# Row sums of squared differences: the end of a row of x loaded last, and y's later loads in five even pieces

**The chip and the metric.** The kernel runs on one core of a Trainium2 chip. The metric is the time of one execution on the device in microseconds (us), from the chip's own clock. The profile comes from one execution each; its span runs from the first to the last instruction and is some 1.3 us shorter than the time. All runs told here are at a granted clock of 1.0.

## The reference

```python
def setup_inputs():
    batch, dim = 1024, 4096
    return {"x": np.random.randn(batch, dim).astype(np.float32),
            "y": np.random.randn(batch, dim).astype(np.float32), "axis": -1}

def reference(x, y, axis):
    return np.sum((x - y) ** 2, axis=axis).astype(np.float32)
```

Each of the 128 partitions holds 8 whole rows, that is 8 x 4096 = 32768 columns of x and as many of y. 33.55 MB must come in, and 4 KB go out.

## The kernel before

All loads are issued by SyncE on one queue, in the order in which they are needed. VectorE subtracts y from x in place as soon as a piece of both has landed, ScalarE squares the difference and sums it (an activation with an accumulator, which is read by a second small instruction), and a row that came in several pieces is completed on VectorE by a reduction over its partial sums. X and Y in SBUF hold six rows each; rows 6 and 7 take the place of rows 0 and 1, so their loads wait for the squares of those. The last 128 columns of row 3 (of y only, in this version) are kept back and loaded last of all; VectorE finishes them alone, with one subtraction and one fused square and sum, while ScalarE finishes row 7. Cuts are marked with dots; the comments are added here.

```python
    xw = [4096, 12288, 8192, 5472, 1280, 960, 320, 160]
    yw = [16256, 8192, 2624, 2784, 1344, 480, 480, 288]
    late, last = 128, 192
    LATE = 3
    halved = (1, 2, 3, 4)          # y loads whose columns are subtracted and squared in halves
    cut = (LATE + 1) * D - late
    ...
    ys += [(N - last, N), (cut, cut + late)]
    ...
    for j, (c0, c1) in enumerate(ys):
        final = j == len(ys) - 1
        wait_loaded(c1, landed_y[j][1])
        for piece in pieces_of(j, c0, c1):
            sub(*piece)                                   # VectorE, L175
            r = piece[0] // D
            if final:
                nc.vector.wait_ge(diffs, n["diffs"])
                nc.vector.tensor_tensor_reduce(...)       # VectorE, L204: the kept-back end of row 3
                continue
            square(*piece, where[piece])                  # ScalarE, L181
            ...
        if j == 4:
            for r in (4, 5, 6):
                complete(r)                               # VectorE, L188
    complete(7)
    nc.sync.wait_ge(sums, n["sums"])
    nc.sync.dma_start(out=ov, in_=results).then_inc(stored, 16)
```

Of the kernel before, what the change touches and what calls it, by code (L numbers as in the profile page):

```python
# [47 lines left out]
def kernel(tc, x, y, axis, out):  # L48
    nc = tc.nc
    P = nc.NUM_PARTITIONS  # L50
    F32 = mybir.dt.float32
    Square = mybir.ActivationFunctionType.Square
    mult, add = mybir.AluOpType.mult, mybir.AluOpType.add

    B, D = x.shape
    R = B // P
    N = R * D


    xv = x.rearrange("(p r) d -> p (r d)", p=P)  # L60
    yv = y.rearrange("(p r) d -> p (r d)", p=P)
    ov = out.rearrange("(p r) -> p r", p=P)


    H = 6 * D
    X = nc.alloc_sbuf_tensor("X", [P, H], F32).ap()
    Y = nc.alloc_sbuf_tensor("Y", [P, H], F32).ap()
    results = nc.alloc_sbuf_tensor("results", [P, R], F32).ap()



    xw = [4096, 12288, 8192, 5472, 1280, 960, 320, 160]
    yw = [16256, 8192, 2624, 2784, 1344, 480, 480, 288]
    late, last = 128, 192
    LATE = 3
    halved = (1, 2, 3, 4)
    cut = (LATE + 1) * D - late
    assert sum(xw) == N and sum(yw) == N - late - last
    xs, c = [], 0
    for w in xw:  # L80
        xs.append((c, c + w))
        c += w
    ys, c = [], 0
    for w in yw:
        ys.append((c, c + w))
        c += w
        if c == cut:
            c += late
    ys += [(N - last, N), (cut, cut + late)]

    prog = Program(nc, tc)
    stored = nc.alloc_semaphore("stored")
    diffs = prog.semaphore("diffs")
    acts = prog.semaphore("acts")
    sums = prog.semaphore("sums")
    n = dict(diffs=0, acts=0, sums=0)

    def home(c0, c1):
        h0 = c0 % H
        return slice(h0, h0 + c1 - c0)  # L100


    landed_x, landed_y = [], []
    freed = []

    def load(landed, src, dst, name, c0, c1):
        sem = prog.semaphore("%s%d" % (name, len(landed)))
        nc.sync.dma_start(out=dst[:, home(c0, c1)], in_=src[:, c0:c1]).then_inc(sem, 16)  # L108
        landed.append(((c0, c1), sem))

    order = []
    have = 0
    for c0, c1 in ys:
        while have < c1:
            order.append((landed_x, xv, X, "x") + xs[len([o for o in order if o[3] == "x"])])
            have = order[-1][5]
        order.append((landed_y, yv, Y, "y", c0, c1))

    todo = list(order)
    load(*todo.pop(0))  # L120
    prog.early(mybir.EngineType.SP)
    while todo and todo[0][5] <= H:
        load(*todo.pop(0))


    row_parts = [[] for _ in range(R)]
    def pieces_of(j, c0, c1):

        pieces = []
        while c0 < c1:  # L130
            e = min(c1, (c0 // D + 1) * D)
            if j in halved:
                h = (c0 + e) // 64 * 32
                pieces.append((c0, h))
                c0 = h
            pieces.append((c0, e))
            c0 = e
        return pieces

    for j, (c0, c1) in enumerate(ys):  # L140
        for piece in pieces_of(j, c0, c1):
            row_parts[piece[0] // D].append(piece)
    parts, where = None, {}
    total = sum(len(p) for p in row_parts if len(p) > 1)
    parts = nc.alloc_sbuf_tensor("parts", [P, total], F32).ap()
    k = 0
    for r, p in enumerate(row_parts):
        for piece in p:
            where[piece] = parts[:, k : k + 1] if len(p) > 1 else results[:, r : r + 1]
            k += len(p) > 1  # L150
    first = {}
    k = 0
    for r, p in enumerate(row_parts):
        if len(p) > 1:
            first[r] = k
            k += len(p)

    def parts_of(r, m):
        return parts[:, first[r] : first[r] + m]

    seen_x = [0]

    def wait_loaded(c1, ysem):

        waits = []
        while seen_x[0] < len(xs) and xs[seen_x[0]][0] < c1:
            waits.append(seen_x[0])
            seen_x[0] += 1
        nc.vector.wait_ge(ysem, 16)
        for k in waits:  # L170
            nc.vector.wait_ge(landed_x[k][1], 16)

    def sub(c0, c1):
        a = X[:, home(c0, c1)]
        nc.vector.tensor_sub(out=a, in0=a, in1=Y[:, home(c0, c1)]).then_inc(diffs, 1)  # L175
        n["diffs"] += 1

    def square(c0, c1, acc):
        a = X[:, home(c0, c1)]
        nc.scalar.wait_ge(diffs, n["diffs"])  # L180
        nc.scalar.activation(out=a, in_=a, func=Square, accum_out=acc).then_inc(acts, 1)  # L181
        n["acts"] += 1

    squared = {}

    def complete(r):
        nc.vector.wait_ge(acts, squared[row_parts[r][-1]])
        nc.vector.tensor_reduce(  # L188
            out=results[:, r : r + 1],
            in_=parts_of(r, len(row_parts[r])),  # L190
            axis=mybir.AxisListType.X,
            op=add,
        ).then_inc(sums, 1)
        n["sums"] += 1

    for j, (c0, c1) in enumerate(ys):
        final = j == len(ys) - 1
        wait_loaded(c1, landed_y[j][1])
        for piece in pieces_of(j, c0, c1):
            sub(*piece)  # L200
            r = piece[0] // D
            if final:
                nc.vector.wait_ge(diffs, n["diffs"])
                nc.vector.tensor_tensor_reduce(  # L204
                    out=Y[:, home(*piece)],
                    in0=X[:, home(*piece)],
                    in1=X[:, home(*piece)],
                    scale=1.0,
                    scalar=parts_of(r, 1),
                    op0=mult,  # L210
                    op1=add,
                    accum_out=results[:, r : r + 1],
                ).then_inc(sums, 1)
                n["sums"] += 1
                continue
            square(*piece, where[piece])
            squared[piece] = n["acts"]
            if r in (0, 1):

                nc.sync.wait_ge(acts, n["acts"])  # L220
                while todo and todo[0][5] <= H + (r + 1) * D:
                    load(*todo.pop(0))
                if r == 1:
                    while todo:
                        load(*todo.pop(0))
        if j == 4:
            for r in (4, 5, 6):
                complete(r)
    complete(7)

    nc.sync.wait_ge(sums, n["sums"])
    nc.sync.dma_start(out=ov, in_=results).then_inc(stored, 16)
    prog.close(nc.sync, stored, 16)
# [35 lines left out]
```

## Time and profile before

| | before |
|---|---|
| time, first three runs | 84.12 us (84.08 to 84.34) |
| the profiled run | 83.96 us, span 82.6 |
| bytes read | 33.55 MB, 406 GB/s over the span |
| loads | 8 of x, 10 of y |
| busy VectorE, ScalarE | 36.8 and 33.4 us |
| last load landed | 80.25 us |
| last reduction began | 80.99 us |

The table is to be read from the bottom up. What counts is when the last bytes arrive and how long the way from there to the last reduction is. The busy shares say nothing here, because both engines stand idle for the first 40 us, until the first long load of y has landed. The prediction below shows the lines. One line of the timeline that it only speaks of is this; its columns are start, length, engine, line, operation, operands, count, and the idle time before with what ended it:

```profile
73.28 4.80 DVE L175 TENSOR_TENSOR X<-X,Y 128x736 f32<-128x736 f32 x6 [0.37 <-DMA Y<-in_y_dram]
```

It shows VectorE working off a lump: the 2784 columns of y landed at 73.25, and six subtractions follow without a pause.

### The profile page before, as it was taken

What the parts mean: (1) busy time and instruction counts of PE and PEld (TensorE: products, weight loads), DVE (VectorE), ACT (ScalarE), POOL (GpSimd) and SP (SyncE); (2) the same over time, 40 slices, a digit from 0 to 9 for tenths busy, and PEclk for the clock granted to TensorE, in tenths of its full rate; (3) what the DMA queues carried; (4) which work ended last, traced back from release to release, by engine and by line L of the source; (5) the groups of instructions that cost most, each with busy time, mean ns of one, the idle gap of its engine ahead of it and who ended that gap; (6) DMA issues with size and microseconds to landing.
All of it is one profiled execution on the core that took longest, in us unless ns stands there. A gap on an engine that the chain in (4) does not pass through costs nothing.

```text
span 82.6 us, 136 instructions
## 1 busy us (share of the span) xinstructions
DVE 36.8 (45%) x27; ACT 33.4 (40%) x41; POOL 0.2 (0%) x4
## 2 busy tenths in 40 slices
DVE  0000000000000000000299999999189996989992
ACT  3300000000000000000000979889896999899991
POOL 0000000000000000000000000000000000000000
DMA  5998998888999991999599699969979799999960
GB/s 127 389 500 381 595 547 381 381 381 381 504 504 504 504 504 63 441 504 504 254 508 508 286 476 508 476 286 508 423 339 509 339 437 440 426 402 416 395 220 2
DMA packets 2736, 33.56 MB, mean 406 GB/s; under 512 B 432, under 2 KB 1328, under 8 KB 1712
## 3 DMA queue, kind: packets, MB, share of 16 engines
q1 hardware_dynamic: 2736, 33.56, 95.9%
HBM read 33.55 MB, written 0.00 MB: 406 GB/s over the span
## 4 chain that ended last, share of the span: by engine, by line
DMA 63%; SPq 16%; DVE 12%; ACT 4%; issue 1%
DMA Y<-in_y_dram 63%; SPq L108 16%; DVE X L175 11%; ACT X L181 4%; DVE Y L204 0%; DVE results L188 0%; SPq L220 0%; DVE results L204 0%
## 5 line engine op out<-in xcount | busy, mean ns | idle before, releaser
L175 DVE TENSOR_TENSOR X<-X,Y 128x2048 f32<-128x2048 f32 (+10 forms) x21 | 36.2, 1780 | 44.3 <-DMA Y<-in_y_dram 44.3
L181 ACT ACTIVATE X<-X 128x2048 f32<-128x2048 f32 (+9 forms) x20 | 31.2, 1559 | 46.1 <-DVE X L175 46.0
L181 ACT ACTIVATION_READ_ACCUMULATOR X<-X 128x1 f32 x20 | 3.7, 186 | 0.0
L181 ACT ACT_TABLE_LOAD x1 | 1.3, 1283 | 1.4 <-PEq L19 1.4
L188 DVE TENSOR_REDUCE results<-parts 128x1 f32<-128x2 f32 (+2 forms) x4 | 0.4, 152 | 0.0
L204 DVE CUSTOM_DVE_ANT_0 Y<-X,parts 128x128 f32<-128x128 f32 x1 | 0.4, 352 | 0.0
L250 POOL MEMSET const-bfloat16-1.0<- 128x1 bf16 x1 | 0.1, 101 | 0.0
L250 POOL MEMSET const-uint8-127<- 128x1 uint8 x1 | 0.1, 101 | 0.0
L250 POOL MEMSET const-float32-0.0<- 128x1 f32 x1 | 0.1, 98 | 0.2 <-issue 0.2
L250 POOL MEMSET const-float32-1.0<- 128x1 f32 x1 | 0.1, 98 | 0.0
L204 DVE DVE_READ_ACCUMULATOR2_ANT results<- 128x1 f32 x1 | 0.1, 83 | 0.0
## 6 DMA issues: line engine op xcount, KB each, us to landing
Y<-in_y_dram SPq DMA_DIRECT2D x1, 8128.0 KB, 39.0
X<-in_x_dram SPq DMA_DIRECT2D x1, 6144.0 KB, 20.2
X<-in_x_dram SPq DMA_DIRECT2D x1, 4096.0 KB, 48.3
Y<-in_y_dram SPq DMA_DIRECT2D x1, 4096.0 KB, 57.5
X<-in_x_dram SPq DMA_DIRECT2D x1, 2736.0 KB, 13.3
X<-in_x_dram SPq DMA_DIRECT2D x1, 2048.0 KB, 7.1
Y<-in_y_dram SPq DMA_DIRECT2D x1, 1392.0 KB, 19.0
Y<-in_y_dram SPq DMA_DIRECT2D x1, 1312.0 KB, 16.1
```

Of the source, the lines that this page charges most:

```text
L108: nc.sync.dma_start(out=dst[:, home(c0, c1)], in_=src[:, c0:c1]).then_inc(sem, 16)
L175: nc.vector.tensor_sub(out=a, in0=a, in1=Y[:, home(c0, c1)]).then_inc(diffs, 1)
L181: nc.scalar.activation(out=a, in_=a, func=Square, accum_out=acc).then_inc(acts, 1)
L188: nc.vector.tensor_reduce(out=results[:, r : r + 1], in_=parts_of(r, len(row_parts[r])), axis=mybir.AxisListType.X, op=add,).then_inc(sums, 1)
L204: nc.vector.tensor_tensor_reduce(out=Y[:, home(*piece)], in0=X[:, home(*piece)], in1=X[:, home(*piece)], scale=1.0, scalar=parts_of(r, 1), ...
L250: nc = _bacc.Bacc("TRN2", target_bir_lowering=False, num_devices=1)
```

## The change

Its intent is to smooth the last fifteen microseconds. The end of row 3 of x is kept back like that of y, so that the last pair of loads is small on both sides. One load of 6816 columns of x runs ahead, and y follows in five loads of about 1350 columns. Each of them, and the 768 columns after them, is subtracted and squared in halves. The number of loads stays at 18.

```diff
--- before.py
+++ after.py
@@ -69,24 +69,25 @@
 
 
 
-    xw = [4096, 12288, 8192, 5472, 1280, 960, 320, 160]
-    yw = [16256, 8192, 2624, 2784, 1344, 480, 480, 288]
-    late, last = 128, 192
+
+    xw = [4096, 12160, 8192, 6816, 768, 608]
+    yw = [16256, 8192, 1344, 1312, 1440, 1376, 1344, 768, 288, 320]
+    late = 128
     LATE = 3
-    halved = (1, 2, 3, 4)
+    halved = (1, 2, 3, 4, 5, 6, 7)
     cut = (LATE + 1) * D - late
-    assert sum(xw) == N and sum(yw) == N - late - last
-    xs, c = [], 0
-    for w in xw:
-        xs.append((c, c + w))
-        c += w
-    ys, c = [], 0
-    for w in yw:
-        ys.append((c, c + w))
-        c += w
-        if c == cut:
-            c += late
-    ys += [(N - last, N), (cut, cut + late)]
+
+    def pieces(widths):
+        spans, c = [], 0
+        for w in widths:
+            spans.append((c, c + w))
+            c += w
+            if c == cut:
+                c += late
+        assert c == N
+        return spans + [(cut, cut + late)]
+
+    xs, ys = pieces(xw), pieces(yw)
 
     prog = Program(nc, tc)
     stored = nc.alloc_semaphore("stored")
@@ -109,12 +110,12 @@
         landed.append(((c0, c1), sem))
 
     order = []
-    have = 0
-    for c0, c1 in ys:
-        while have < c1:
-            order.append((landed_x, xv, X, "x") + xs[len([o for o in order if o[3] == "x"])])
-            have = order[-1][5]
-        order.append((landed_y, yv, Y, "y", c0, c1))
+    xk = 0
+    for piece in ys:
+        while xk < len(xs) and (xs[xk][0] < piece[1] if xk < len(xs) - 1 else piece == ys[-1]):
+            order.append((landed_x, xv, X, "x") + xs[xk])
+            xk += 1
+        order.append((landed_y, yv, Y, "y") + piece)
 
     todo = list(order)
     load(*todo.pop(0))
@@ -160,12 +161,15 @@
 
     seen_x = [0]
 
-    def wait_loaded(c1, ysem):
+    def wait_loaded(c1, ysem, final):
 
         waits = []
-        while seen_x[0] < len(xs) and xs[seen_x[0]][0] < c1:
+        while seen_x[0] < len(xs) - 1 and xs[seen_x[0]][0] < c1:
             waits.append(seen_x[0])
             seen_x[0] += 1
+        if final:
+            assert seen_x[0] == len(xs) - 1
+            waits.append(seen_x[0])
         nc.vector.wait_ge(ysem, 16)
         for k in waits:
             nc.vector.wait_ge(landed_x[k][1], 16)
@@ -195,7 +199,7 @@
 
     for j, (c0, c1) in enumerate(ys):
         final = j == len(ys) - 1
-        wait_loaded(c1, landed_y[j][1])
+        wait_loaded(c1, landed_y[j][1], final)
         for piece in pieces_of(j, c0, c1):
             sub(*piece)
             r = piece[0] // D
@@ -223,7 +227,7 @@
                 if r == 1:
                     while todo:
                         load(*todo.pop(0))
-        if j == 4:
+        if j == 6:
             for r in (4, 5, 6):
                 complete(r)
     complete(7)
```

## The prediction

> **What bounds the kernel now.** I began with the page: its busy shares, the forty slices and the chain that ended last.
>
> ```profile
> DVE 36.8 (45%) x27; ACT 33.4 (40%) x41; POOL 0.2 (0%) x4
> DMA  5998998888999991999599699969979799999960
> GB/s 127 389 500 381 595 547 381 381 381 381 504 504 504 504 504 63 441 504 504 254 508 508 286 476 508 476 286 508 423 339 509 339 437 440 426 402 416 395 220 2
> DMA 63%; SPq 16%; DVE 12%; ACT 4%; issue 1%
> ```
>
> The two engines that compute work less than half of the span, the 16 DMA engines from the second slice to the last but one. Most of the chain is DMA. The 16% of SyncE's queue is issue time that lies beside transfers already queued: in the windows 40 to 50 us and 50 to 60 us, where it falls, the DMA moved 442 and 432 GB/s, no less than elsewhere. So the kernel is 33.55 MB at the rate of the DMA, and then a tail. The end of the chain shows the tail:
>
> ```profile
> 66.94 13.12 DMA Y<-in_y_dram
> 80.05 0.02 issue
> 80.08 0.57 DVE X L175 x2
> 80.65 0.03 issue
> 80.67 0.35 DVE Y L204
> 81.03 0.01 DVE results L204
> 81.03 0.12 DVE results L188
> ```
>
> The chain names 80.05 us. That is the last load but one, 192 columns of y. By the trace's landing records the last, 128 columns, lands at 80.25; VectorE had not come to it then. From the data at 80.05 follow two subtractions, the fused square and sum, and the reduction of row 7, which is through at 81.15; the store of the results takes the rest up to 82.6. Which engine is late just before? The timeline answers for both:
>
> ```profile
> 79.58 1.06 DVE L175 TENSOR_TENSOR X<-X,Y 128x288 f32<-128x288 f32 x3 [0.15 <-DMA Y<-in_y_dram]
> 79.97 0.19 ACT L181 ACTIVATION_READ_ACCUMULATOR X<-X 128x1 f32 x1
> 80.08 0.44 ACT L181 ACTIVATE X<-X 128x288 f32<-128x288 f32 x1
> 80.42 0.19 ACT L181 ACTIVATION_READ_ACCUMULATOR X<-X 128x1 f32 x1
> 80.52 0.35 ACT L181 ACTIVATE X<-X 128x192 f32<-128x192 f32 x1
> 80.77 0.19 ACT L181 ACTIVATION_READ_ACCUMULATOR X<-X 128x1 f32 x1
> 80.95 0.08 DVE L204 DVE_READ_ACCUMULATOR2_ANT results<- 128x1 f32 x1
> 80.99 0.16 DVE L188 TENSOR_REDUCE results<-parts 128x1 f32<-128x8 f32 x1
> ```
>
> VectorE still waits for data at 79.58, so it has caught up. ScalarE does not wait: its activations follow each other from about 72.9 us, with only their accumulator reads between. The 192 columns were subtracted at 80.08 + 0.36 = 80.44, and ScalarE takes them at 80.52, at most some 0.06 us late. It ends at 80.96, VectorE's fused operation and its accumulator read end at 81.03: the two branches into the last reduction are nearly even.
>
> **What the Trainium skill says.** "DMA: Bandwidth & Descriptors", section "Where 436 GB/s comes from", puts the ceiling at 435 GB/s. The trace agrees: the 8192 columns of y before 60.27 us took 9.72 us, that is 8192 x 128 x 4 B / 9.72 us = 431 GB/s. There is no rate left to win on large loads. Section "Why small descriptors are slow (HBM only)" speaks of a fixed overhead per packet; the gaps between landings below show a small one. "VectorE: DVE Perf Modes", section on the TRN2 errata, gives (N+151)/0.96 ns for an fp32 tensor_tensor: 2291 ns for 2048 columns, where the trace has 2287, and 291 for 128, where it has 285. "ScalarE: Activation LUTs", section "What ACT_TABLE_LOAD costs", gives 186 ns + 0.833 per column and an overlap of about 93 ns: 1892 for 2048, where the trace has 1910.
>
> **The change, part by part.**
>
> *Loads.* Before there are 8 of x and 10 of y, after 7 and 11: 18 both times, with the same bytes. I took the gaps between landings, in order of issue, as what each load costs: 8192 columns 9.72 us, 5472 6.49, 2624 3.17, 1344 1.61, 960 1.16, 480 0.60, 320 0.41, 288 0.40, 192 0.26, 160 0.23, 128 0.20. A line through the 13 gaps after y's 8192 columns is 0.038 us + 1.180 ns per column, with no point off by more than 0.03. In such a model the end of the stream depends on the number of loads and the sum of columns, and neither changes: the last landing stays at 80.25. If I take the measured gaps for each new size instead, interpolating where there is none, the 13 new ones add to 20.05 us against 19.99 for the old, but they begin 0.15 us sooner, since the 128 columns of x moved to the end come out of the second load: 80.16. So the transfers give 0 to 0.1 us.
>
> *When the loads are issued.* After the fifth load everything waits for the squares of row 1 (at 53.4 us) in both kernels: the new third load of x also reaches beyond row 0's room. Data runs until 60.27, and the last load was wholly issued at 72.98, 7 us before it landed. With 13 loads behind the wait again, I expect no starvation.
>
> *Rows 4 and 5*, four halves of 2048: unchanged, 8.90 us of VectorE from 60.15 instead of 60.29, free at 69.05.
>
> *The middle.* Five y loads of 1344, 1312, 1440, 1376, 1344 replace 2624, 2784, 1344. x's 6816 land first, at 60.12 + 0.04 + 8.04 = 68.2. Then y lands at 69.82, 71.41, 73.15, 74.81 and 76.43 by the line. VectorE needs for two halves about 2 x (0.07 us + 1.0417 ns x half), the 0.07 being what is left of the 8.90 us for four 2048s after their duration: 1.54, 1.51, 1.64, 1.57 and 1.54. Every piece is done before the next arrives. Before, the 2784 came in one lump at 73.25 and gave 4.80 us of subtraction in a row, and a backlog for ScalarE. Now VectorE is done at 78.0 with these and has paid its three reductions (some 0.2 us, from 77.99 to 78.18 before) by 78.2; the next data come at 78.3. ScalarE's pitch of about 0.75 us per 672 (76.61 to 77.35 to 78.11) keeps up with 1.6 us for two. This removes waiting that lay under the DMA; the part of it at the end was 0.06 us.
>
> *The end.* x 768, y 768, x 608, y 288, y 320, x 128, y 128 land at 77.38, 78.32, 79.08, 79.46, 79.87, 80.06 and 80.25. VectorE: 768 in halves 78.35 to 79.3; 288 from 79.49; 320 from 79.90, free for the next at 79.90 + 0.07 + 0.333 = 80.30; the last 128 from 80.30 instead of 80.36 (80.08 + 0.28). That is 0.06 us off the VectorE branch, with one subtraction of 128 after the last data where there were 192 and 128. But ScalarE now squares 320 columns last, not 192. Its data are ready at 79.90 + 0.49 = 80.39, it starts at 80.42, and at the old distance from start to end of accumulator read (80.96 - 80.52 = 0.44 for 192, plus 128 x 0.833 ns = 0.55) it ends at 80.97, where it was 80.96. So the reduction starts where it did, near 81.0. If the loads really end 0.1 us sooner, all of it moves by 0.1.
>
> Sum: transfers 0 to -0.1, tail 0 to -0.06, both branches considered. I take -0.08 of 84.12, that is 84.04 us.
>
> **The rivals.**
> 1. *The even pieces pay more*: the ScalarE backlog costs more than the trace of one run shows, and the tail shrinks from 0.74 us (80.25 to 80.99) to the 0.65 of a bare subtraction and fused operation (0.28 + 0.28 + 0.08), while fewer loads under 2 KB a row (four where there were seven) quicken the stream by 0.15. For it: gaps of 192 and 160 columns at 1.37 and 1.44 ns per column against 1.19 for large ones. Against it: 128, 128, 288 and 320 remain, which pay the same. Time: 83.8.
> 2. *A new wait*: the final pair now needs x and y of the cut, two loads of 512 B a row one after the other, and y's 320 before them. If a small load takes longer to complete than the gap of 0.20 says, or VectorE falls behind with 15 small pieces in a row, the end moves out by up to 0.2: 84.3. Against it: the one 128-column load of before showed just that 0.20.
> 3. *The queue runs short*, because 6816 columns of x hold it and 12 loads wait behind. SyncE's issues took up to 5.6 us in the timeline; I read that as a full queue, which is no loss. If it were one, up to 0.5 us: 84.6. I give it little.
>
> **Range and chances.** The three runs of before lie from 84.08 to 84.34, and a profiled run took 83.96; that noise is more than the effect. So 84.04, from 83.75 to 84.30 in 8 of 10. Two per cent is 1.68 us; the whole way from the last landing to the last reduction is only 0.74, and the stream is at the measured 431 GB/s, so faster by 2% is nearly ruled out (0.01). Slower by 2% would need the queue to run empty (0.01).
>
> **What would show it.** The landings: the last within 0.1 us of 80.25, and the gaps on the line. VectorE: an idle stretch before most of the y pieces from 69.8 to 78.3, where it had one run of 4.80 us, and hence more waits for DMA; that they grow is no loss. ScalarE: gaps between its activations in that stretch. The tail: one subtraction before the fused operation, and a reduction near 80.9 to 81.0 that waits for ScalarE. It would be wrong if the last landing moves by more than 0.2 us, if the gap after x's 6816 columns shows idle DMA engines, or if the store at the end takes another time than the 1.4 us of before.

## The result

The changed kernel took 84.23 us (median of 6 runs, 84.13 to 84.30), the old one 84.11 in the same rounds. The ratio is 1.0008, with a 95% interval from 0.9995 to 1.0022. Ratios here are the mean time of one kernel's runs over that of the other's in the same rounds, so they are not quite the ratio of the medians. The forecast was 84.04 in a range from 83.75 to 84.30.

The page of the profile after, the lines of busy time, DMA and chain:

```profile
DVE 37.2 (45%) x29; ACT 34.0 (41%) x45; POOL 0.2 (0%) x4
DMA  5999998888999999299969979997999989999950
DMA 70%; ACT 13%; DVE 12%; SPq 2%; issue 1%
```

The two engines are busy for 0.4 and 0.6 us longer, which is two subtractions and two activations more. The DMA engines are as full as before. What differs is the last line: 13% of the chain is now ScalarE, where it was 4%. The end of the chain after, each line with its start, its length and what it is:

```profile
54.73 18.70 DMA Y<-in_y_dram
73.43 0.02 issue
73.45 0.90 DVE X L179
74.35 0.02 issue
74.37 6.95 ACT X L185 x20
81.32 0.02 issue
81.34 0.16 DVE results L192
```

Before, the chain left the DMA at 80.05 and went through VectorE. Now it leaves the DMA at 73.43 and then runs for 6.95 us through ScalarE alone: 20 instructions, one after the other, with no wait long enough for this view. The last reduction is released by ScalarE at 81.32. The timeline shows what ScalarE does last:

```profile
70.12 8.24 DVE L179 TENSOR_TENSOR X<-X,Y 128x672 f32<-128x672 f32 x10 [0.98 <-DMA Y<-in_y_dram]
...
80.24 0.44 ACT L185 ACTIVATE X<-X 128x288 f32<-128x288 f32 x1
80.59 0.18 ACT L185 ACTIVATION_READ_ACCUMULATOR X<-X 128x1 f32 x1
80.75 0.47 ACT L185 ACTIVATE X<-X 128x320 f32<-128x320 f32 x1
80.95 0.35 DVE L208 CUSTOM_DVE_ANT_0 Y<-X,parts 128x128 f32<-128x128 f32 x1
81.12 0.19 ACT L185 ACTIVATION_READ_ACCUMULATOR X<-X 128x1 f32 x1
81.23 0.08 DVE L208 DVE_READ_ACCUMULATOR2_ANT results<- 128x1 f32 x1
81.34 0.16 DVE L192 TENSOR_REDUCE results<-parts 128x1 f32<-128x8 f32 x1
```

The 320 columns landed at 80.20 by the landing records. VectorE's subtraction of them took until about 80.72, ScalarE's activation and accumulator read until 81.31, and the reduction follows at 81.34: 1.14 us from that landing. Where ScalarE is pressed, an activation starts 0.10 us after the start of the accumulator read before it (80.14 to 80.24). Before the 320 columns it is 0.16 (80.59 to 80.75), so ScalarE could have begun about 0.06 us earlier and waited for VectorE. The chain's long way through ScalarE from 73.43 therefore isn't what the end hangs on; that is the landing at 80.20. VectorE is not far behind either: its accumulator read starts at 81.23, and in the traces below in which VectorE ends last the reduction starts within 0.01 us of the start of that read. So at most some 0.11 us of the end is due to ScalarE alone. The first of these lines is VectorE in the middle: its ten halves take 8.24 us from 70.12, with no pause long enough to be listed.

The landing records of these two traces, in us, with the latest of the 16 DMA engines and, in the last column, the distance between the first and the last engine:

```
                          last of 16    first to last engine
before  first load             7.12            0.23
        y's 8192 columns      60.27            0.21
        last load             80.25            0.24
after   first load             7.21            0.39
        y's 8192 columns      60.22            0.38
        last load             80.54            0.53
```

The changed kernel's stream ends 0.29 us later, but its 16 engines are already 0.39 us apart after the first load, which is the same load in both kernels. So the first question was whether the stream had got slower at all.

### The profile page after: what moved, and what is told of

The parts are those of the page before. It is cut to its first block, busy times and chain, and to the rows that moved or that the text cites. A ratio compares the mean times of both kernels' runs of the same rounds, so it can differ in the third digit from the quotient of the medians.

```text
span 83.0 us, 141 instructions
## 1 busy us (share of the span) xinstructions
DVE 37.2 (45%) x29; ACT 34.0 (41%) x45; POOL 0.2 (0%) x4
## 3 DMA queue, kind: packets, MB, share of 16 engines
HBM read 33.55 MB, written 0.00 MB: 404 GB/s over the span
## 4 chain that ended last, share of the span: by engine, by line
DMA 70%; ACT 13%; DVE 12%; SPq 2%; issue 1%
DMA Y<-in_y_dram 70%; ACT X L185 13%; DVE X L179 12%; SPq L109 2%; DVE results L192 0%; SPq L224 0%
## 5 line engine op out<-in xcount | busy, mean ns | idle before, releaser
L179 DVE TENSOR_TENSOR X<-X,Y 128x672 f32<-128x672 f32 (+10 forms) x23 | 36.5, 1639 | 44.2 <-DMA Y<-in_y_dram 43.9
L185 ACT ACTIVATE X<-X 128x672 f32<-128x672 f32 (+9 forms) x22 | 31.6, 1437 | 45.9 <-DVE X L179 45.9
```

The lines of the kernel that those rows point to most:

```text
L179: nc.vector.tensor_sub(out=a, in0=a, in1=Y[:, home(c0, c1)]).then_inc(diffs, 1)
L185: nc.scalar.activation(out=a, in_=a, func=Square, accum_out=acc).then_inc(acts, 1)
```

## The experiments

Two theories stood against each other. **The stream**: the end moves with the last landing, which the number of loads and the sum of columns set, plus how the 16 engines happen to drift apart. **The pieces**: VectorE and ScalarE are nearly saturated over the last ten microseconds, and the sizes, places and order of the pieces set how long after the last landing ScalarE is through with its last one. The runs were made in three calls, each on one chip, with the kernel before timed in the same rounds (medians of 11 runs). It took 84.15 us beside the first four told here, 84.14 beside "without the halves", "the middle in three", "fifteen more loads" and "a shorter last piece", and 84.08 beside the other two.

### The old kernel again

No edit.

> The unchanged kernel against itself: ratio 1.000 within 0.2%. It gives a second trace on the chip of the three others. My theory is that the 0.29 us by which the last load landed later after the change (80.54 against 80.25) lies mostly in how far the 16 DMA engines drift apart in a run, because the first load, the same in both, already landed with 0.39 us between its first and last engine instead of 0.23. Then this trace may show a spread of 0.4 to 0.5 at the end and a last landing up to 80.5 without any change. The rival, that the change itself slows the stream, expects the spread of 0.24 and 80.25 again.

It took 84.14 us, ratio 0.9997 (0.9980 to 1.0014). Its trace is of an execution of 84.34 us: the last load landed at 80.67, with 0.43 us between first and last engine, and the reduction began at 81.38, 0.71 later. So the same kernel has a last landing of 80.25 in one trace and 80.67 in another. The first profile had fallen on a fast execution (83.96 us). The spread is the one expected, the landing is later than the 80.5 expected. What single traces show of the stream's end is not exact to better than 0.4 us, more than the whole effect sought.

### The changed kernel again

No edit.

> The changed kernel a second time, beside the old one on the same chip. Drift theory: the last landing is within 0.1 us of that of before_again, and the time within 0.1 us. Rival (the stream is slower by the change): last landing 0.2 to 0.3 us later than that of before_again, x's 6816 columns again taking 8.2 us where 38 ns plus 1.18 ns per column give 8.08.

It took 84.21 us, ratio 1.0002 (0.9986 to 1.0018). The last load landed at 80.50, 0.17 before that of the old kernel's trace on the same chip, and x's 6816 columns took 8.07 us, not 8.21. The rival's forecast (0.2 to 0.3 us later, and 8.2 us again for x's 6816 columns) failed, and the timed runs show no difference, so nothing here shows the stream slower by the change. The drift theory's own mark, 0.1 us between the two landings, was missed too. The distance from the last landing to the reduction was 0.80 us in the first trace after and 0.78 now, against 0.74 and 0.71 before. That distance repeats to 0.03 us, the landing does not. From here on I read the distance from the traces and the sum from the timed runs.

### Only x's end last

```diff
-    xw = [4096, 12160, 8192, 6816, 768, 608]
-    yw = [16256, 8192, 1344, 1312, 1440, 1376, 1344, 768, 288, 320]
+    xw = [4096, 12160, 8192, 5472, 1280, 960, 320, 160]
+    yw = [16256, 8192, 2624, 2784, 1344, 480, 480, 288, 192]
-    halved = (1, 2, 3, 4, 5, 6, 7)
+    halved = (1, 2, 3, 4)
-        if j == 6:
+        if j == 4:
```

> Only the end of row 3 of x comes last; all other sizes as before: 19 loads instead of 18. Load-count theory: one load more, +0.04 us in the last landing, and the tail as before, so 0 to +0.1 us. Rival (two loads of 512 B a row one after the other at the end are slow): +0.2 us and gaps over 0.3 us for the last two loads.

It took 84.08 us, ratio 0.9989 (0.9972 to 1.0006). The end of its chain of waits:

```profile
73.31 7.41 DMA Y<-in_y_dram
80.73 0.02 issue
80.75 0.30 DVE X L179
81.05 0.02 issue
81.08 0.35 DVE Y L208
81.43 0.01 DVE results L208
81.44 0.07 DVE results L192
```

The chain leaves the DMA with the very last load (80.73) and goes through one subtraction and the fused operation. VectorE's 192 columns are done when the last 128 land; ScalarE begins on them then (80.73) and is through at 81.19, before VectorE. The distance from landing to reduction is 0.63 us (81.35 - 80.73), where it was 0.71 to 0.74; the tail was expected to stay as it was. The last two loads of 512 B a row took 0.22 and 0.19 us, so they aren't slow: that rival falls. By this trace, the part saves about 0.1 us of the tail and costs one load.

### Only the new sizes

```diff
-    xw = [4096, 12288, 8192, 5472, 1280, 960, 320, 160]
-    yw = [16256, 8192, 2624, 2784, 1344, 480, 480, 288]
-    late, last = 128, 192
+    xw = [4096, 12288, 8192, 6816, 768, 608]
+    yw = [16256, 8192, 1344, 1312, 1440, 1376, 1344, 768, 288]
+    late, last = 128, 320
-    halved = (1, 2, 3, 4)
+    halved = (1, 2, 3, 4, 5, 6, 7)
-        if j == 4:
+        if j == 6:
```

(The edit is against the kernel before.)

> Only the new sizes with their halves; x's end of row 3 comes with the rest: 17 loads. Load-count theory: one load fewer, -0.04 us in the last landing; ScalarE's last piece of 320 columns makes up for it in the tail, so within 0.1 us of before. Rival (the small even pieces slow the stream or the engines): +0.2 us or more, as slow as the changed kernel.

It took 84.39 us, ratio 1.0024 (1.0007 to 1.0041). That is 0.24 us over before, outside what I had expected, and the interval leaves out 1. The end of its chain:

```profile
54.99 18.55 DMA Y<-in_y_dram
73.55 0.02 issue
73.57 0.90 DVE X L175
74.47 0.02 issue
74.50 6.86 ACT X L181 x20
81.36 0.02 issue
81.38 0.16 DVE results L188
```

The last load landed at 80.42, with one load fewer and earlier than in the old kernel's trace beside it, and still the reduction came at 81.38: a distance of 0.96 us. ScalarE sets it, but by little: VectorE's accumulator read started at 81.27, 0.11 us before the reduction. VectorE is late as well, because it subtracts the last 128 columns after the 320: its fused operation starts 0.57 us after the last landing (80.99 - 80.42), where it was 0.42 before. ScalarE's last 320 columns landed at 80.24, and from there to the reduction it is 1.14 us, as in the changed kernel (80.20 to 81.34, and 80.13 to 81.28 in its second trace). But here they landed only 0.18 us before the end of the stream. In the full change it is 0.34 and 0.37, since 128 columns of x come after them. So the new sizes cost about 0.24 us by themselves, and x's end, put last, takes 0.18 of that back (84.39 to 84.21; the means of six runs each differ by 0.185, with a standard error of 0.06). The two parts of the change work against each other.

### Without the halves

```diff
-    halved = (1, 2, 3, 4, 5, 6, 7)
+    halved = (1,)
```

(This edit and all that follow are against the changed kernel.)

> The changed kernel with only rows 4 and 5's load halved, the six y loads after it whole. The stream ends where it did. Theory (ScalarE's queue of pieces sets the tail): ScalarE gets its 768-column piece about 0.5 us later and is still busy with it when the last 320 columns are ready, so the end moves out by 0.2 us, to about 84.4. Rival (only the last landing counts, the halves lie under the DMA and buy nothing): 84.2, or less, since there are six fewer accumulator reads.

It took 84.37 us, ratio 1.0019 (0.9999 to 1.0038), with the reduction 0.92 us after the last landing. ScalarE's timeline:

```profile
78.20 1.32 ACT L185 ACTIVATE X<-X 128x1344 f32<-128x1344 f32 x1
79.43 0.18 ACT L185 ACTIVATION_READ_ACCUMULATOR X<-X 128x1 f32 x1
79.52 0.83 ACT L185 ACTIVATE X<-X 128x768 f32<-128x768 f32 x1
...
80.78 0.45 ACT L185 ACTIVATE X<-X 128x320 f32<-128x320 f32 x1
```

A whole piece reaches ScalarE only when the whole of it is subtracted (the last 1344 columns at 78.17), so ScalarE starts its 768 columns at 79.52, where the two halves of the changed kernel on the other chip started at 79.13 and 79.65. Before the 320 columns it is pressed now (its accumulator read before them starts at 80.68, the activation at 80.78), so the end no longer depends on their landing but on what ScalarE had to do before. In time it is about 0.15 us over the changed kernel's 84.21 to 84.23, each beside an old kernel of 84.11 to 84.15. That points to the pieces, though the interval just touches 1.

### The middle in three

```diff
-    yw = [16256, 8192, 1344, 1312, 1440, 1376, 1344, 768, 288, 320]
+    yw = [16256, 8192, 2624, 2784, 1408, 768, 288, 320]
-    halved = (1, 2, 3, 4, 5, 6, 7)
+    halved = (1, 2, 3, 4, 5)
-        if j == 6:
+        if j == 4:
```

> The changed kernel with y's five even loads merged to 2624, 2784 and 1408, as before, x's 6816 columns still ahead of them. The stream has two loads fewer and ends 0.08 us sooner. Theory (the five even loads only make good what x's one long load takes): VectorE gets its first pair at about 71.3 instead of 69.9 and never catches up; ScalarE ends 1.4 us later, so about 85.6. Rival (the even loads are a gain by themselves, the DMA bounds all): 84.1 to 84.3.

It took 85.53 us, ratio 1.0157 (1.0135 to 1.0179). VectorE's timeline:

```profile
71.49 2.96 DVE L179 TENSOR_TENSOR X<-X,Y 128x1312 f32<-128x1312 f32 x2 [2.40 <-DMA Y<-in_y_dram]
74.83 4.87 DVE L179 TENSOR_TENSOR X<-X,Y 128x736 f32<-128x736 f32 x6 [0.38 <-DMA Y<-in_y_dram]
...
82.53 0.16 DVE L192 TENSOR_REDUCE results<-parts 128x1 f32<-128x8 f32 x1 [0.35 <-ACT X L185]
```

The stream ended early, at 80.30, and the reduction waited 2.23 us more, for ScalarE. VectorE stood idle for 2.40 us before its first piece, since x's 6816 columns and then 2624 of y had to land. With x's one long load ahead, then, the five even loads are needed to pay for it; the old kernel had neither. Whether even loads of y gain anything with x's old loads was not run.

### Fifteen more loads

```diff
-    xw = [4096, 12160, 8192, 6816, 768, 608]
+    xw = [4096] + [760] * 16 + [8192, 6816, 768, 608]
```

> The changed kernel with x's second load of 12160 columns cut into 16 loads of 760, under no computation. The cost of a load is measured by itself. Load-count theory: 15 x 0.038 = 0.57 us later at the end, about 84.8. Rival 1 (the 0.038 us is only an effect of short rows at the end of the stream): under 0.1 us. Rival 2 (SyncE's 0.44 us per issue or the full queue holds it back): over 1 us.

It took 85.24 us, ratio 1.0119 (1.0096 to 1.0141), 1.01 us over the first result of the changed kernel. The direction is right, the size isn't: 1.0 us is what rival 2 had named, so it has to be judged by the trace. From the landing of the first load to that of the sixteenth piece 15.36 us passed; the one load of 12160 columns took 14.39 in the first trace after. That is 0.97 / 15 = 0.065 us for a load. The gaps after these loads are as before, so nothing was held back later. SyncE issued a load every 0.4 to 0.9 us and was through with the sixteen at 10.6 us, while the last of them landed at 22.68, so its issues did not hold them back, and rival 2 falls.

### Fifteen more loads, aligned

```diff
-    xw = [4096, 12160, 8192, 6816, 768, 608]
+    xw = [4096] + [768] * 15 + [640, 8192, 6816, 768, 608]
```

> Fifteen more loads as in fifteen_more_loads, but of 768 columns (and one of 640), so that each row of each load starts at a multiple of 256 bytes. There the sixteen loads took 15.36 us from first landing to last, 0.40 more than the line through the old gaps gives (16 x 0.935 = 14.96), and the gaps changed with the place in a pattern of eight. If rows that start off 256 bytes are the cause, the sixteen take 14.95 to 15.05 us now and the time is about 84.8. If the number of loads alone is the cause, and costs more than 0.038 us each here, they take 15.3 again and the time is 85.2.

It took 85.32 us, ratio 1.0137 (1.0109 to 1.0165). The sixteen took 15.48 us (22.86 - 7.39), 0.073 us for each load more. Where the rows start isn't the cause. A load of 768 columns of x among others of x took 0.98 us here; the same size, x and y in turn near the end, took 0.93 twice in the same trace. Why a load costs more in the one place than in the other stays open.

### A shorter last piece for ScalarE

```diff
-    yw = [16256, 8192, 1344, 1312, 1440, 1376, 1344, 768, 288, 320]
+    yw = [16256, 8192, 1344, 1312, 1440, 1376, 1344, 768, 480, 128]
```

> The changed kernel with the last two pieces of row 7 of 480 and 128 columns instead of 288 and 320. Rival (ScalarE's last piece sets the end, so a short one helps): 0.1 us faster than the changed kernel. Theory (ScalarE's backlog, the sum of what it has yet to do when a piece arrives, sets the end): the 480 columns come 0.2 us later than the 288 did and hold both engines; VectorE ends 0.2 and ScalarE 0.4 us later: about 84.6.

It took 84.63 us, ratio 1.0055 (1.0036 to 1.0075). The end of its chain of waits:

```profile
79.97 0.67 DVE X L179
80.64 0.02 issue
80.67 1.00 ACT X L185 x4
81.66 0.02 issue
81.69 0.16 DVE results L192
```

The piece before the last is now 480 columns. It lands later, holds VectorE until 80.64, and ScalarE, which had to wait for it, then takes 1.00 us for both pieces. The distance from landing to reduction is 1.19 us. The shorter last piece doesn't help: what counts is the longest way from any landing to the end, and now it starts at the 480 columns, which landed at 79.95, 1.74 us before the reduction.

### Only x's end last, once more

The same kernel as in the third experiment.

> The kernel of x_cut_only once more, against the old one, on what may be another chip: its ratio was 0.9989 with an interval from 0.9972 to 1.0006, so whether it beats both kernels is open. Theory (the late x takes 0.15 us of transfer from in front of ScalarE's last piece, at the price of one load of 0.04 us): 0.05 to 0.1 us faster than before, 84.05. Rival (no gain): 84.15.

It took 84.12 us, ratio 0.9995 (0.9975 to 1.0015). The distance from landing to reduction was again 0.63 us (81.11 - 80.48). The shorter tail repeats, but a gain in time isn't shown: the two medians are 0.07 below and 0.04 above those of the old kernel beside it, and both intervals hold 1. No version was found that beats the old kernel.

The traces together, without the two of the fifteen loads, with the landing and the reduction in us of each trace and the time as a median:

| kernel | last landing | reduction | distance | time | old kernel beside it |
|---|---|---|---|---|---|
| before | 80.25 | 80.99 | 0.74 | 84.11 | |
| before again | 80.67 | 81.38 | 0.71 | 84.14 | 84.15 |
| after | 80.54 | 81.34 | 0.80 | 84.23 | 84.11 |
| after again | 80.50 | 81.28 | 0.78 | 84.21 | 84.15 |
| only x's end last | 80.73 | 81.35 | 0.63 | 84.08 | 84.15 |
| the same again | 80.48 | 81.11 | 0.63 | 84.12 | 84.08 |
| only the new sizes | 80.42 | 81.38 | 0.96 | 84.39 | 84.15 |
| without the halves | 80.43 | 81.35 | 0.92 | 84.37 | 84.14 |
| the middle in three | 80.30 | 82.53 | 2.23 | 85.53 | 84.14 |
| 480 and 128 at the end | 80.50 | 81.69 | 1.19 | 84.63 | 84.14 |

## Why the prediction was right

The measured 84.23 us lies in the range, and "within 2%" had been given 0.98. In part that is luck of the range: it was set from the noise and held the unchanged kernel (84.11 to 84.15) too, so it doesn't confirm the small gain that was forecast. By its own steps:

- **The stream is the bound and the change leaves it alone.** Right. Its end depends on loads and columns, and the changed kernel's trace on the same chip as the old one's ended 0.17 us sooner, within what one kernel varies by itself (80.25 and 80.67). But the forecast of "0 to -0.1 us" for the transfers was finer than the traces can show, and its starting point of 80.25 came from a fast execution. One reading beside it was off: none of SyncE's issue time in the chain falls between 40 and 50 us; all but 0.33 us of it lies between 53.4 and 66.9. The conclusion stands, as the DMA moved 429 GB/s from 60.3 to 66.8.
- **The line of 0.038 us and 1.180 ns per column.** Right for the gaps that it was fitted to and for the new sizes near the end (6816 columns: 8.08 by the line, 8.07 and 8.21 in the two traces after). As the cost of a load in general it was mis-sized: 0.065 and 0.073 us where it was measured by itself. The gaps show a cost per load; whether it is the overhead per packet that the prediction cites, no run here shows.
- **No starvation by the issues.** Right: 15 more loads and their issues delayed nothing but by their own transfer. (What the prediction calls the new third load of x is the fourth.)
- **The middle.** Right that both engines keep up, wrong in what would show it. The "4.80 us in a row" was not all the lump's: 3.26 us of it were, the rest was the next load. VectorE was to have an idle stretch before most of the y pieces and more waits for DMA, and ScalarE gaps. By the forecast's terms VectorE's ten halves should take 10 x 0.07 + 6816 x 1.0417 ns = 7.8 us and took 8.24, so the pauses were some 0.04 us each, and the listed waits for DMA fell from 5 to 3. ScalarE waited once, 0.17 us before 74.37, and its next six activations took 4.83 us (74.37 to 79.20) where 4160 columns at 0.833 ns (the forecast's figure) and six times 0.2 us, the surcharge seen in the traces, come to an estimated 4.67. The even pieces run both engines at nearly their full rate; there is little slack in them, and none to save where the stream sets the end. That the even pieces removed waiting, as the forecast put it, is not what the runs show: they make good the late start that x's one long load brings (the middle in three).
- **The end.** Right in its mechanism: ScalarE's 320 columns set the reduction (the chain names it), and the 0.55 us from start to end of its accumulator read was 0.56 (80.75 to 81.31). From the landing of the 320 columns to ScalarE's end 1.10 us were forecast (79.87 to 80.97) and 1.11 measured (80.20 to 81.31). The distance from the last landing, estimated at 80.97 - 80.25 = 0.72, was 0.78 to 0.80: the reduction starts 0.03 us after ScalarE's end, and the two loads of 128 columns landed within 0.34 to 0.37 us, not 0.38. VectorE's branch was not 0.06 us shorter either: from the last landing to the start of the fused operation it was 0.42 us before (80.25 to 80.67) and is 0.41 and 0.38 (80.54 to 80.95, 80.50 to 80.88).
- **The sign.** The sum of -0.08 us came out as +0.12 and +0.06 in the two sets of medians, neither clear of noise. Rival 1, 83.8 by even pieces, has the reverse of what the new sizes do alone. What the forecast didn't see is that the change is two parts of opposite sign: about +0.24 for the sizes alone and some -0.18 for x's end when added to them. The order of 0.1 us for x's end (0.15 us of transfer moved behind ScalarE's last piece) was there to be worked out from the gaps.

## What to carry to other kernels

When the DMA sets the pace and two engines follow it closely, the number to watch is the way from the second engine's last landing through both engines to the end, 1.14 us here, less what of the stream comes after that landing. The other engine's way has to be checked beside it; here it ended within 0.11 us of the first. Split the tail of a trace into the last landing and the distance from there to the last instruction: here the first wandered by 0.4 us between executions of one kernel, while the second repeated within 0.03 and ranked the variants that differ only in the tail. A change that does two things at once should be run in its two halves, since "same" can be a gain and a loss.

## What the Trainium skill lacked or had wrong

- "DMA: Bandwidth & Descriptors", section "Where 436 GB/s comes from", says that for transfers from HBM to SBUF the HBM side binds at about 358 GB/s. Here one core read 8192 columns of y at 431 GB/s and 33.55 MB at 406 over the whole span, so the figure of about 435 is the one that held. The sentence lacks a condition that the page's section "Measured" has: about 358 is each core's share when both cores of a pair stream, and a single core reached 425 GB/s with 16 MB.
- The same page, section "Measured", has 64 KB at 0.95 us and 138 GB/s for a transfer issued from GpSimd. Loads of that size, queued behind others on SyncE's queue, landed 0.16 to 0.24 us apart (65.5 KB in that time is 270 to 410 GB/s). It has no figure for what one more load costs on a full queue: 0.065 to 0.073 us early in the kernel, about 0.04 by the line near the end.
- No page tells how far the 16 DMA engines drift apart within one kernel: 0.23 us after the first load in one trace, 0.37 to 0.51 in all others, and the last landing of one kernel at 80.25 or 80.67 us.
- "ScalarE: Activation LUTs", section "What ACT_TABLE_LOAD costs", gives a time for the activation and none for its accumulator. With one, a second instruction of 0.186 us reads it, and pieces of 384 columns followed each other every 0.52 us (79.13 to 79.65), 0.20 us over the 0.833 ns per column, where the page's 186 ns less 93 of overlap would give 0.09.
